# Issuing the first load of a streaming kernel ahead of the program's opening barrier

## The chip, the cores and the metric

The kernel runs on one core of one Trainium2 chip. The metric is the device time of one execution in microseconds (us). A run is one execution of the program. Runs are called fast, or slow when they lie over 1.5% above the fastest run of the same kernel. A ratio below is the mean time of one kernel's fast runs over that of the other's fast runs of the same rounds, so it is not quite the ratio of the medians that are quoted beside it. The profile is one execution; its span is about 2 us shorter than the device time.

## The reference

```python
batch, seq, d_model, r = 16, 512, 768, 16      # x: 16 x 512 x 768 fp32, A: 768 x 16, B: 16 x 768
def reference(x, A, B, scale):                 # scale = 0.5
    lora = np.matmul(np.matmul(x, A), B)
    return (x + scale * lora).astype(np.float32)
```

x is 25.2 MB and so is the output. A and B are 48 KB each.

## The kernel before

x is cut into 8 groups of 3.1 MB (128 partitions of 24,576 bytes). For each group ScalarE casts x to fp16, VectorE transposes it in 32 by 32 blocks of 32-bit words, TensorE multiplies with A (spread into a block-diagonal matrix `a_diag`), ScalarE spreads the result into `y_diag`, TensorE multiplies with B (`b_rep`), and VectorE adds the product to x in place. The tensor goes out from the same buffer. Six buffers hold x. All transfers are issued by SP (SyncE), and so stand in one queue:

```python
    xs = [const.tile([P, G, D], fp32, name=f"x_{i}") for i in range(X_BUFS)]   # X_BUFS = 6
...
    def load(g):
        nc.sync.dma_start(out=xs[g % X_BUFS], in_=view(x2, g)).then_inc(loaded[g], 16)

    def sync_program():
        load(0)
        nc.sync.dma_start(
            out=a32.rearrange("i (b r) -> i b r", b=NB),
            in_=A.rearrange("(b i q) r -> i b (q r)", i=Q, q=2),
        ).then_inc(a_in, 16)
        nc.sync.dma_start(out=b32, in_=B).then_inc(b_in, 16)
        for g in range(1, X_BUFS):
            load(g)
        for g in range(NG - 1):
            nc.sync.wait_ge(added, 4 * (g + 1) + 2)
            nc.sync.dma_start(out=view(out2, g), in_=xs[g % X_BUFS]).then_inc(...)
            if g == len(freed) - 1:
                for n in range(X_BUFS, NG):
                    nc.sync.wait_ge(freed[n - X_BUFS], 16)
                    load(n)
...
    def vector_program():
        ...                                   # A and B to fp16, a_diag, b_rep: waits for a_in and b_in
        turn(0, 0, G // 2)._wait_ge(ready, 1)
        turn(0, G // 2, G // 2)._wait_ge(ready, 2)
        for g in range(NG):
            if g + 1 < NG:
                turn(g + 1, 0, G)._wait_ge(ready, 2 * g + 4)      # the transpose
            for s in range(0, G, 2):
                ...                                               # x += product, four times
...
    with tc.tile_critical(no_gpsimd_drain=True):
        sync_program(); pool_program(); scalar_program(); vector_program(); tensor_program()

    nc.sync.dma_start(out=view(out2, NG - 1), in_=xs[(NG - 1) % X_BUFS])
```

The program begins with a barrier that nobody wrote here: GpSimd sets four constants, every engine reports, and GpSimd releases them. Only then does SP reach `load(0)`.

## Time and profile before

The time before is 124.38 us (median of 4 runs, 124.25 to 124.48).

| What | Before | Where it is read |
|---|---|---|
| SP reaches the barrier / is released | 0.00 / 0.65 us | the records of single instructions in the trace |
| first load issued | 0.94 us, for 0.38 us | timeline |
| first packet of that load | 1.95 us | the DMA packets in the trace |
| first load landed | 11.6 us | the DMA's semaphore in the trace, and ScalarE's wait |
| from one landing to the next | 7.3 us | the same |
| last store issued / stores before it landed | 106.3 / 114.1 us | timeline / semaphore |
| last packet | 121.0 us | the DMA packets |

The profile's page of the kernel before: its span, the busy time of each engine, the granted TensorE clock, the DMA's busy share in tenths and its rate in 40 equal slices, the one queue's share of the 16 engines' span, and the chain of work that ended last.

```profile
span 122.2 us, 888 instructions
PE 50.6 (41%) x323; PEld 30.0 (25%) x323; DVE 84.2 (69%) x48; ACT 55.9 (46%) x42; POOL 4.9 (4%) x9
...
PEclk9999999976999999999999999999999999655555
DMA  5899999999999999999999999999999999999992
GB/s 129 378 459 346 418 451 418 435 435 418 443 426 418 451 426 410 451 451 394 475 418 402 459 426 410 443 435 410 459 418 451 435 410 451 427 402 467 427 410 121
...
q1 hardware_dynamic: 2736, 50.43, 97.2%
...
DVE 44%; PE 21%; DMA 14%; ACT 6%; SPq 1%; issue 1%
```

The queue is busy for 97.2% of the engines' span, and no engine of compute comes near that: VectorE (DVE) has 69%. The last line seems to say otherwise, with VectorE first in the chain that ended last. The timeline of the kernel before, at its start and at its end (start in us, length, engine, line, operation, output<-input; "SPq" is SP's sequencer, that is, the issue of a transfer):

```profile
0.94 0.38 SPq L92 DMA_DIRECT2D x_61<-in_x_dram  x1
1.37 0.43 SPq L96 DMA_DIRECT2D a_71<-in_A_dram  x1
1.85 0.46 SPq L100 DMA_DIRECT2D b_72<-in_B_dram  x1
2.35 0.42 SPq L92 DMA_DIRECT2D x_62<-in_x_dram  x1
...
11.62 5.41 ACT L132 CAST xh_67<-x_61 128x3072 f16<-128x3072 f32 x2 [9.44 <-DMA x_61<-in_x_dram]
```

```profile
104.03 1.75 DVE L186 TENSOR_TENSOR x_62<-x_62,lora_ps_80 128x1536 f32<-128x1536 f32 x1
106.28 0.33 SPq L242 DMA_DIRECT2D out_dram<-x_62  x1
```

SP's own waits in the kernel before (who waited for whom: us in total, times, longest):

```profile
SPq L273 <- DMA out_dram<-x_62: 14.8, 1, 14.8
```

The last store is issued at 106.3 us and SP then waits 14.8 us for it, although one 3.1 MB transfer takes 7.3 us. The other half is queueing: the store before it lands only at 114.1 us, 7.8 us after the last one is issued. So the end hangs on the queue.

### The profile page before, as it was taken

To read this page: it belongs to the slowest core of one execution; us is meant where nothing else is said; L and a number is where in the kernel's file an instruction comes from. 1 tells how busy PE (TensorE), PEld (TensorE's weight loads), DVE (VectorE), ACT (ScalarE), POOL (GpSimd) and SP (SyncE) were. 2 spreads that over 40 slices of the span, in tenths; PEclk is the share of its full clock that TensorE was granted. 3 is DMA by queue.
4 is the path that set the end of the run, shared out by engine and by line. 5 is a ranking of instruction groups with operands and counts; after the bars stand their busy time and mean duration, and the time that the engine had idled before them with its cause. 6 is when DMAs were issued, how large, how long until landed. Compare 5 with 4: busy or idle time off the path is not lost.

```text
span 122.2 us, 888 instructions
## 1 busy us (share of the span) xinstructions
PE 50.6 (41%) x323; PEld 30.0 (25%) x323; DVE 84.2 (69%) x48; ACT 55.9 (46%) x42; POOL 4.9 (4%) x9
## 2 busy tenths in 40 slices
PE   0000406747744674294374458429437545000000
PEld 0000004512531352182153226217214422000000
DVE  0001993099999999999999999999999559600000
ACT  4001956989459629908934099991400310000000
POOL 7800000000000000000000000000000000000000
PEclk9999999976999999999999999999999999655555
DMA  5899999999999999999999999999999999999992
GB/s 129 378 459 346 418 451 418 435 435 418 443 426 418 451 426 410 451 451 394 475 418 402 459 426 410 443 435 410 459 418 451 435 410 451 427 402 467 427 410 121
DMA packets 2736, 50.43 MB, mean 413 GB/s; under 512 B 672, under 2 KB 672, under 8 KB 688
## 3 DMA queue, kind: packets, MB, share of 16 engines
q1 hardware_dynamic: 2736, 50.43, 97.2%
HBM read 25.26 MB, written 25.17 MB: 413 GB/s over the span
## 4 chain that ended last, share of the span: by engine, by line
DVE 44%; PE 21%; DMA 14%; ACT 6%; SPq 1%; issue 1%
DVE xt L155 19%; PE y_ps L213 15%; DMA x_62<-in_x_dram 14%; DVE x_62 L186 8%; DVE x_61 L186 5%; PE lora_ps_80 L227 5%; ACT xh_68 L132 4%; DVE x_66 L186 3%; DVE x_65 L186 3%; DVE x_63 L186 3%; DVE x_64 L186 3%; ACT y_diag L143 1%; PE lora_ps_79 L227 1%; SPq L100 0%; SPq L96 0%
## 5 line engine op out<-in xcount | busy, mean ns | idle before, releaser
L213 PE MATMUL y_ps<-xt,a_diag 128*128 128x256 f16 x192 | 24.2, 282 | 5.9 <-DVE xt L155 5.9
L227 PE MATMUL lora_ps_79<-b_rep,y_diag 128*128 128x512 f16 (+1 forms) x64 | 13.8, 340 | 27.9 <-ACT y_diag L143 14.4
L143 ACT ACTIVATE y_diag<-y_ps 32x256 f16<-32x256 f32 x32 | 12.0, 375 | 25.7 <-PE y_ps L213 25.4
L213 PEld LDWEIGHTS y_ps<-xt,a_diag 128*128 128x128 f16 x192 | 18.9, 99 | 11.1 <-DVE xt L155 6.6
L155 DVE STREAM_TRANSPOSE xt<-xh_68 128x3072 uint32<-128x3072 uint32 x4 | 13.5, 3378 | 6.0 <-ACT xh_68 L132 5.2
L227 PE MATMUL lora_ps_80<-b_rep,y_diag 128*128 128x512 f16 (+1 forms) x64 | 13.8, 340 | 6.7 <-DVE x_61 L186 1.7
L132 ACT CAST xh_67<-x_61 128x3072 f16<-128x3072 f32 (+1 forms) x3 | 10.7, 3603 | 12.6 <-DMA x_61<-in_x_dram 12.6
L155 DVE STREAM_TRANSPOSE xt<-xh_67 128x3072 uint32<-128x3072 uint32 (+1 forms) x5 | 13.6, 2728 | 0.8 <-PE y_ps L213 0.8
L227 PEld LDWEIGHTS lora_ps_79<-b_rep,y_diag 128*128 128x128 f16 x64 | 5.1, 99 | 35.8 <-issue 16.9
L132 ACT CAST xh_68<-x_62 128x6144 f16<-128x6144 f32 x2 | 10.6, 5312 | 2.5 <-DMA x_62<-in_x_dram 2.5
L227 PEld LDWEIGHTS lora_ps_80<-b_rep,y_diag 128*128 128x128 f16 x64 | 5.8, 101 | 13.3 <-DVE x_61 L186 2.5
L186 DVE TENSOR_TENSOR x_62<-x_62,lora_ps_79 128x1536 f32<-128x1536 f32 x4 | 7.0, 1740 | 2.8 <-PE lora_ps_79 L227 2.8
L164 DVE CAST a_74<-a_71 32x384 f16<-32x384 f32 x1 | 0.3, 348 | 11.9 <-DMA a_71<-in_A_dram 11.9
L186 DVE TENSOR_TENSOR x_62<-x_62,lora_ps_80 128x1536 f32<-128x1536 f32 x4 | 7.0, 1744 | 0.0
L186 DVE TENSOR_TENSOR x_61<-x_61,lora_ps_80 128x1536 f32<-128x1536 f32 x4 | 7.0, 1741 | 0.0
L186 DVE TENSOR_TENSOR x_61<-x_61,lora_ps_79 128x1536 f32<-128x1536 f32 x4 | 6.9, 1728 | 0.0
L198 PE MATMUL lora_ps_79<-a_74,rep 32*128 32x384 f16 x1 | 0.5, 497 | 12.3 <-DVE a_74 L164 12.3
L132 ACT CAST xh_67<-x_63 128x6144 f16<-128x6144 f32 x1 | 5.3, 5313 | 0.4 <-DMA x_63<-in_x_dram 0.4
L132 ACT CAST xh_68<-x_64 128x6144 f16<-128x6144 f32 x1 | 5.3, 5312 | 0.0
L132 ACT CAST xh_68<-x_66 128x6144 f16<-128x6144 f32 x1 | 5.3, 5312 | 0.0
L132 ACT CAST xh_67<-x_65 128x6144 f16<-128x6144 f32 x1 | 5.3, 5312 | 0.0
L186 DVE TENSOR_TENSOR x_63<-x_63,lora_ps_80 128x1536 f32<-128x1536 f32 x2 | 3.5, 1742 | 0.0
(23 smaller groups left out, 35.5 us busy)
## 6 DMA issues: line engine op xcount, KB each, us to landing
x_61<-in_x_dram SPq DMA_DIRECT2D x2, 3072.0 KB, 12.6
x_62<-in_x_dram SPq DMA_DIRECT2D x2, 3072.0 KB, 15.8
out_dram<-x_61 SPq DMA_DIRECT2D x2, 3072.0 KB, 19.5
out_dram<-x_62 SPq DMA_DIRECT2D x2, 3072.0 KB, 16.6
x_63<-in_x_dram SPq DMA_DIRECT2D x1, 3072.0 KB, 23.7
x_64<-in_x_dram SPq DMA_DIRECT2D x1, 3072.0 KB, 30.5
x_65<-in_x_dram SPq DMA_DIRECT2D x1, 3072.0 KB, 37.2
x_66<-in_x_dram SPq DMA_DIRECT2D x1, 3072.0 KB, 44.0
```

The costliest lines, as they stand in the source:

```text
L132: i = nc.scalar.copy(out=xh[g % 2][:, rows, :], in_=xs[g % X_BUFS][:, rows, :])
L143: i = nc.scalar.mul(out=y_diag[q, :, q], in_=y_ps[q, :, :], mul=sc)
L155: i = nc.vector.transpose(out=xt[:, rows, :].rearrange("p s w -> p (s w)"), in_=xh[g % 2][:, rows, :].rearrange("p s d -> p (s d)").bitcas ...
L164: nc.vector.tensor_copy(out=a16, in_=a32)._wait_ge(a_in, 16).then_inc(setup_dve, 1)
L186: nc.vector.tensor_tensor(out=rows, in0=rows, in1=lora_ps[n % 2], op=mybir.AluOpType.add)._wait_ge(ups, n + 1).then_inc(added, 1)
L198: nc.tensor.matmul(a_ps, rep, a16, start=True, stop=True)._wait_ge(setup_dve, 1).then_inc(setup_pe, 1)
L213: i = nc.tensor.matmul(y_ps, a_diag[:, k, :], xt_mm[:, :, k // 2, :, k % 2], start=(k == 0), stop=(k == 2 * NB - 1),)
L227: i = nc.tensor.matmul(flat[:, ds(c0, w)], y_diag[:, s + k, :], b_rep[:, ds(c0 - k * D, w)], start=True, stop=True,)
```

## The change

The intent: SP does nothing useful in the opening barrier, and the load of the first group depends on nothing that the barrier orders. So its issue is put in front of SP's part in the barrier. The program's first block is made before the framework places its tiles, so the buffer of that load gets a fixed address of its own.

```diff
-    xs = [const.tile([P, G, D], fp32, name=f"x_{i}") for i in range(X_BUFS)]
+    x_0 = nc.alloc_sbuf_tensor("x_0", [P, G, D], fp32).ap()
+    xs = [x_0] + [const.tile([P, G, D], fp32, name=f"x_{i}") for i in range(1, X_BUFS)]
...
     def sync_program():
+        symbolic, nc._always_lower_symbolic_ap = nc._always_lower_symbolic_ap, False
         load(0)
+        nc._always_lower_symbolic_ap = symbolic
+
+        now, first = nc.cur_bb.bb.instructions, nc.main_func.blocks[0].instructions
+        at = next(
+            k for k, i in enumerate(first)
+            if i.engine == mybir.EngineType.SP and isinstance(i, mybir.InstDrain)
+        )
+        first.insert(at, now.pop())
         nc.sync.dma_start(
             out=a32.rearrange("i (b r) -> i b r", b=NB),
```

## The prediction

> **What bounds the kernel now.** The DMA queue, from end to end. The page gives the DMA digit 9 in 38 of 40 slices, 97.2% of the 16 engines' span, 50.43 MB at 413 GB/s. All loads and stores stand in one queue, and the landings in the trace are a steady beat: the first load of x at 11.6 us, the next ones at 19.2, 26.5, 33.9, 41.2, 48.5, then the first two stores at 55.8 and 63.1, one 3.1 MB transfer per 7.3 us. The packets of that queue run from 1.95 us to 121.02 us with no hole between. The last store is issued at 106.3 us (timeline), when the store before it has not landed (114.1 us), so it stands about 7.8 us behind others. The page's "chain that ended last" (VectorE 44%) therefore misleads: VectorE could finish about 7 us later and the end would not move. The Trainium skill ("DMA: Bandwidth & Descriptors", section on queues, rings and completion order) says that each engine consumes its descriptors in ring order; the landings agree.
>
> **What the change does.** It takes the first load's issue from 0.94 us to the front of the program, before SP's part in the opening barrier. The trace shows SP's first instruction at 0.00 us and the barrier's release reaching SP at 0.65 us, then two small steps and the issue at 0.94 us. The issue takes 0.38 us, and the first packet moves 0.63 us after it ends. (The same page, "Latency and other measured facts", states about 0.6 us for this; the trace agrees.) Nothing is added: the same transfers, sizes and queue. The order of instructions shows only this one moved; the other engines have identical rows. SP now reaches the barrier at about 0.43 us instead of 0.01 us, but GpSimd, which gathers it, is itself ready only at 0.53 us, so I expect the release at 0.61 us to stay, or slip by at most 0.1 us. The loads of A, B and x1 then go out one issue earlier (about 0.43 us); they queue behind x0 anyway.
>
> **On the critical path.** The queue starts about 0.9 us earlier (first packet at about 1.0 us instead of 1.95) and stays full: x0 takes about 8 us to move, and x1 would be issued at about 1.9 us. Every landing should move by the same 0.9 us, and the end too, since all the stores have slack (the last one 7.8 us) and the compute chain starts earlier as well. Gain: 0.94 us at most, about 0.9 us expected, 0.7% of the time.
>
> **Predicted time:** 123.5 us, range 123.1 to 124.1. Faster by over 2%: 0.01; within 2%: 0.98; slower by over 2%: 0.01.
>
> **What would show it.** First packet at about 1.0 us; x0 landed at about 10.7 us, x1 at 18.3; last packet at about 120.1; span about 121.3; the bytes and the mean 7.3 us beat unchanged; the barrier's release still near 0.6 to 0.7 us; VectorE's and ScalarE's busy times unchanged. The wait of the last store, about 14.8 us, stays.
>
> **What would make it wrong.** (a) SP's drain in the barrier waits for the load itself: then the other engines start late, up to about 10 us, and A, B and x1 are issued after x0, a hole in the queue of a microsecond or two: no gain, or a loss. (b) The first packets, which already take 1.85 us against 0.91 later, ramp more slowly so early in the program, and eat half the gain. (c) The load is the first instruction SP runs and begins later than its drain did, so that the clock of the measurement starts with it and the gain shrinks. (d) The gain is only a few times the spread of runs (124.25 to 124.48), so two medians may show 0.5 or 1.2 us.

## The result

The changed kernel takes 123.43 us (median of 4 runs, 123.18 to 123.67) against 124.38 us; the ratio is 0.9924, with a 95% interval of 0.9897 to 0.9951. Repeated on another chip with six runs it took 123.30 us against 124.31 us, ratio 0.9914 (0.9895 to 0.9934). The page of the changed kernel:

```profile
span 121.3 us, 888 instructions
PE 52.1 (43%) x323; PEld 30.6 (25%) x323; DVE 84.2 (69%) x48; ACT 55.9 (46%) x42; POOL 4.9 (4%) x9
...
PEclk9999999965699999999999999999999999975555
DMA  7999999999999999999999999999999999999991
GB/s 227 421 392 419 397 478 413 397 478 421 397 478 405 413 470 413 413 454 430 413 446 438 413 438 446 413 438 438 421 438 438 413 446 438 413 446 438 413 454 73
...
q1 hardware_dynamic: 2736, 50.43, 97.8%
...
DVE 44%; PE 22%; DMA 13%; ACT 6%; SPq 1%; issue 1%
```

The DMA row has moved at its two ends alone: the first 3 us carry 227 GB/s where they carried 129, and the last 3 us carry 73 where they carried 121. The timeline of the changed kernel, at its start and its end, and SP's wait for the last store:

```profile
0.00 0.38 SPq L94 DMA_DIRECT2D x<-in_x_dram  x1
0.99 0.34 SPq L107 DMA_DIRECT2D a_70<-in_A_dram  x1
1.38 0.73 SPq L111 DMA_DIRECT2D b_71<-in_B_dram  x1
2.16 0.41 SPq L94 DMA_DIRECT2D x_61<-in_x_dram  x1
...
10.41 5.41 ACT L143 CAST xh_66<-x 128x3072 f16<-128x3072 f32 x2 [8.18 <-DMA x<-in_x_dram]
```

```profile
103.87 1.75 DVE L197 TENSOR_TENSOR x_61<-x_61,lora_ps_79 128x1536 f32<-128x1536 f32 x1
106.12 0.33 SPq L253 DMA_DIRECT2D out_dram<-x_61  x1
```

```profile
SPq L284 <- DMA out_dram<-x_61: 14.1, 1, 14.1
```

| us from the span's start | Before | After | Earlier by |
|---|---|---|---|
| first load issued | 0.94 | 0.00 | 0.94 |
| first packet | 1.95 | 1.00 | 0.94 |
| x0 landed | 11.59 | 10.39 | 1.20 |
| x1 landed | 19.22 | 18.06 | 1.16 |
| last load of x landed | 77.73 | 76.44 | 1.29 |
| last store but one landed | 114.12 | 113.25 | 0.87 |
| last packet of all | 121.02 | 120.04 | 0.98 |
| last addition on VectorE ended | 105.78 | 105.62 | 0.16 |

The queue moved as a whole by about 0.9 to 1.3 us, and the span became 0.87 us shorter (122.16 and 121.29 us). A landing here is the last of 16 engines (the trace has 16 packets of 4 bytes, for the semaphore, after each transfer), so it carries a few tenths of scatter.

The last row of the table is a small surprise. VectorE's chain began 1.16 us earlier, with ScalarE's cast of the second group, but ended only 0.16 us earlier. The chain of work that ended last shows where it lost its lead. First the kernel before, then the changed one (start, us, what):

```profile
24.59 3.38 DVE xt L155
27.97 3.31 DVE x_61 L186 x2
...
31.33 0.82 PE lora_ps_80 L227 x4
32.15 2.69 PE y_ps L213 x24
```

```profile
23.43 3.38 DVE xt L166
26.81 3.32 DVE x L197 x2
...
30.17 1.46 PE lora_ps_79 L238 x4
31.63 3.05 PE y_ps L224 x24
```

The same matmuls took 1.46 and 3.05 us in place of 0.82 and 2.69, which is 1.0 us. From 30 to 40 us the clock granted to TensorE was 1.00 before and 0.89 after (mean over that stretch): the trace has it at half from 26.04 to 29.45 us before, and from 25.44 to 32.27 us after. (The 9s of the PEclk row before 22 us only mean that no record of the clock stands there.) The Trainium skill's page "TensorE: Matmul & The Clock Gate", part 1, says that the array is throttled by default and that activity releases it, with a phase that varies from run to run; the traces agree in that the half clock lies among the first rounds of matmuls and elsewhere in each (30.27 to 33.69 us in the repeat of the changed kernel below), but no run here shows what sets it. The lead was lost at no cost to the end, as a chain with slack allows. That is the second sign that the chain does not set the end.

### The profile page after: what moved, and what is told of

Read it like the earlier page. It is cut to its first block, busy times and chain, and to the rows that moved or that the text cites. A ratio compares the mean times of both kernels' runs of the same rounds, so it can differ in the third digit from the quotient of the medians.

```text
span 121.3 us, 888 instructions
## 1 busy us (share of the span) xinstructions
PE 52.1 (43%) x323; PEld 30.6 (25%) x323; DVE 84.2 (69%) x48; ACT 55.9 (46%) x42; POOL 4.9 (4%) x9
## 4 chain that ended last, share of the span: by engine, by line
DVE 44%; PE 22%; DMA 13%; ACT 6%; SPq 1%; issue 1%
DVE xt L166 19%; PE y_ps L224 16%; DMA x_61<-in_x_dram 13%; DVE x_61 L197 8%; DVE x L197 5%; PE lora_ps_79 L238 5%; ACT xh_67 L143 4%; DVE x_65 L197 3%; DVE x_63 L197 3%; DVE x_64 L197 3%; DVE x_62 L197 3%; ACT y_diag L154 1%; PE lora_ps_78 L238 1%; SPq L111 1%; SPq L107 0%
## 5 line engine op out<-in xcount | busy, mean ns | idle before, releaser
L224 PE MATMUL y_ps<-xt,a_diag 128*128 128x256 f16 x192 | 24.8, 287 | 5.8 <-DVE xt L166 5.8
L238 PE MATMUL lora_ps_78<-b_rep,y_diag 128*128 128x512 f16 (+1 forms) x64 | 14.1, 346 | 27.9 <-ACT y_diag L154 14.1
L238 PE MATMUL lora_ps_79<-b_rep,y_diag 128*128 128x512 f16 (+1 forms) x64 | 14.4, 351 | 6.1 <-DVE x_61 L197 1.7
L143 ACT CAST xh_66<-x 128x3072 f16<-128x3072 f32 (+1 forms) x3 | 10.7, 3604 | 10.3 <-DMA x<-in_x_dram 10.3
L197 DVE TENSOR_TENSOR x_61<-x_61,lora_ps_78 128x1536 f32<-128x1536 f32 x4 | 7.0, 1741 | 2.8 <-PE lora_ps_78 L238 2.8
L175 DVE CAST a_73<-a_70 32x384 f16<-32x384 f32 x1 | 0.3, 349 | 10.8 <-DMA a_70<-in_A_dram 10.8
L197 DVE TENSOR_TENSOR x_61<-x_61,lora_ps_79 128x1536 f32<-128x1536 f32 x4 | 7.0, 1744 | 0.0
L197 DVE TENSOR_TENSOR x<-x,lora_ps_79 128x1536 f32<-128x1536 f32 x4 | 7.0, 1741 | 0.0
L197 DVE TENSOR_TENSOR x<-x,lora_ps_78 128x1536 f32<-128x1536 f32 x4 | 6.9, 1729 | 0.0
L209 PE MATMUL lora_ps_78<-a_73,rep 32*128 32x384 f16 x1 | 0.5, 496 | 11.2 <-DVE a_73 L175 11.2
L197 DVE TENSOR_TENSOR x_62<-x_62,lora_ps_79 128x1536 f32<-128x1536 f32 x2 | 3.5, 1742 | 0.0
```

The lines of the kernel that those rows point to most:

```text
L143: i = nc.scalar.copy(out=xh[g % 2][:, rows, :], in_=xs[g % X_BUFS][:, rows, :])
L175: nc.vector.tensor_copy(out=a16, in_=a32)._wait_ge(a_in, 16).then_inc(setup_dve, 1)
L197: nc.vector.tensor_tensor(out=rows, in0=rows, in1=lora_ps[n % 2], op=mybir.AluOpType.add)._wait_ge(ups, n + 1).then_inc(added, 1)
L209: nc.tensor.matmul(a_ps, rep, a16, start=True, stop=True)._wait_ge(setup_dve, 1).then_inc(setup_pe, 1)
L224: i = nc.tensor.matmul(y_ps, a_diag[:, k, :], xt_mm[:, :, k // 2, :, k % 2], start=(k == 0), stop=(k == 2 * NB - 1),)
L238: i = nc.tensor.matmul(flat[:, ds(c0, w)], y_diag[:, s + k, :], b_rep[:, ds(c0 - k * D, w)], start=True, stop=True,)
```

## The experiments

The theory (the queue): one DMA queue is full from its first packet to its last, so the end is the first packet plus a constant, and the gain is the 0.94 us by which the first packet came earlier. The rivals: the VectorE chain that ended last sets the end, and gains because x0 is there earlier (the chain); or the buffer's place outside the framework brings part of the gain (the placement).

### The change again, as a yardstick

No edit. The first four runs of the changed kernel lay in two groups (123.18 and 123.23, 123.63 and 123.67 us), so it was repeated.

> The changed kernel once more, as a yardstick on this chip and for the spread. Queue theory (the end is set by one full DMA queue, so the gain is how much earlier its first packet moves, 0.94 us): ratio to before 0.992 to 0.993. If its runs fall into two groups again (123.2 and 123.65 in the first four), the profile of this run tells which part of the queue's time differs.

123.30 us (6 runs, 123.10 to 123.44), ratio 0.9914. The two groups did not come again, so there was nothing to explain.

### The placement alone

```diff
-    xs = [const.tile([P, G, D], fp32, name=f"x_{i}") for i in range(X_BUFS)]
+    x_0 = nc.alloc_sbuf_tensor("x_0", [P, G, D], fp32).ap()
+    xs = [x_0] + [const.tile([P, G, D], fp32, name=f"x_{i}") for i in range(1, X_BUFS)]
```

> The buffer x_0 outside the framework, but the first load issued where it was before. Queue theory: 124.4 us, ratio 0.999 to 1.001, first packet at 1.95 us. Rival (the placement of the buffer itself brings part of the gain): ratio below 0.998.

124.34 us, ratio 1.0001 (0.9980 to 1.0022); the first packet is at 1.95 us. The placement brings nothing, to within the 0.2% of the interval, where the change brings 0.8 to 0.9%: that rival is out.

### The queue's start moved the other way, by five times as much

```diff
     def sync_program():
+        nc.sync.wait_ge(pool_done, 2)
         load(0)
```

> The kernel before, with SP made to wait ahead of its first load until GpSimd has done its setup at 5.76 us, so that the whole queue starts 4.8 to 4.9 us later. Queue theory: time rises by all of it, to 129.2 us (slope 1.0 us per us of start), with the beat between landings unchanged at 7.3 us. If there were slack anywhere between the queue's start and the end, it would rise by less.

129.00 us (4 runs, 128.87 to 129.15), ratio 1.0374 (1.0349 to 1.0399). The first packet came at 6.80 us, 4.85 us later than before, and the time rose by 4.69 us: 0.97 us for each us of start. The page's DMA row of this run shows the empty start and a queue that is full afterwards:

```profile
DMA  0099989999999999999999999999999999999993
```

The expectation was 129.2 us; the 0.2 us that is missing is about the scatter of single runs. This run delays the queue and the chain alike, so it measures the slope and does not tell the two apart. The next two do.

### VectorE made slower, by 3.4 and by 10.1 us

The transpose of the last group is done two times, or four times, the result being the same (`delay` is a semaphore that orders the repeats):

```diff
+                extra = 1 if g + 1 == NG - 1 else 0        # 3 in the second run
+                for k in range(extra):
+                    nc.vector.wait_ge(*((delay, k) if k else (ready, 2 * g + 4)))
+                    nc.vector.transpose(out=xt..., in_=xh[(g + 1) % 2]...).then_inc(delay, 1)
+                if extra:
+                    nc.vector.wait_ge(delay, extra)
                 turn(g + 1, 0, G)._wait_ge(ready, 2 * g + 4)
```

> The changed kernel with VectorE's transpose for the last group done twice: 3.4 us more VectorE work on the chain that the profile says ended last. Queue theory: VectorE's last addition ends at about 109 us, still before the queue gets to the last store (113.3 us), so the time stays at 123.4 us (ratio to before 0.992). Rival (the VectorE chain sets the end): 3.4 us longer, 126.8 us.

123.61 us (4 fast runs, 123.37 to 124.05), ratio 0.9952 (0.9928 to 0.9977). The last addition ended at 110.6 us where it ended at 105.6 in the changed kernel, so 5 us later: 3.4 us for the repeat, the rest in slower rounds of matmuls. The end hardly moved: by 0.3 us against the yardstick, or 0.4% by the two ratios (0.9952 against 0.9914). SP's wait for the last store shrank by the same 5 us, from 14.1 us to this:

```profile
SPq L294 <- DMA out_dram<-x: 9.1, 1, 9.1
```

> The same with that transpose done four times: 10.1 us more VectorE work. Queue theory: the last addition ends at about 115.8 us and the last store is issued at about 116.3 us, 3.1 us after the queue ran empty at 113.2 us and with about 1 us from issue to first packet, so the end moves by about 4 us: 127.4 us. Rival (the VectorE chain sets the end): 10.1 us longer, 133.5 us.

One run was fast, at 127.61 us; three were slow, at 129.54 to 130.04 us. The fast one is 4.3 us over the yardstick (123.30 us), where the queue theory said about 4 and the chain theory 10.1. The profile fell on a slow run, and its chain shows matmuls of the last group at 4.16 us in place of 2.69:

```profile
103.36 1.46 PE lora_ps L248 x4
104.82 4.16 PE y_ps L234 x24
```

The trace has the clock at half from 94.11 to 107.77 us. There is no trace of the fast run to set beside it, so why the others were slower is not settled. With one fast run there is no interval. The two runs together rule out the chain as what bounds the kernel: 5 us of delay were free, and 10.1 us or more cost 4.3. How much slack it has can be estimated from the traces. Where the last store is late (this one, three loads ahead, and A and B later, below), the last packet comes 8.3 us after its issue. In the changed kernel it comes at 120.04 us, so an issue up to 111.7 us should be free; it came at 106.1, which makes some 5.6 us of slack.

### Three loads ahead of the barrier

If one load ahead is good, are three better?

```diff
     # x_0, x_1 and x_2 get fixed addresses
-        load(0)
+        for g in range(3):
+            load(g)
...
-        first.insert(at, now.pop())
+        for g in range(3):
+            first.insert(at, now.pop())
...
-        for g in range(1, X_BUFS):
+        for g in range(3, X_BUFS):
             load(g)
```

> The first three loads of x ahead of the barrier instead of one. Queue theory: the first packet stays at 1.0 us and the queue is full either way, so the time is that of the changed kernel, ratio to before 0.992 (to within 0.002), although SP comes to the barrier about 0.9 us later and all other engines start that much later. Rival (the issue of each load, or the start of the engines, is on the critical path): two more issues of 0.45 us each ahead bring either a further 0.9 us of gain or 0.9 us of loss.

133.11 us (6 runs, 130.78 to 135.17), ratio 1.0576 (1.0521 to 1.0631) from its two fast runs, 130.78 and 132.24 us. No theory expected a loss of some 8 us against the changed kernel (9.8 us by the median, which counts the slow runs). The page's DMA row of this run (a slow one) has holes, one of which is empty for a whole slice in the row of rates, and the timeline shows when VectorE could begin:

```profile
DMA  7999999999999928905999989799999999996885
GB/s 230 446 423 438 438 409 453 357 409 446 431 416 446 394 119 357 475 0 238 475 305 409 453 386 468 275 438 446 423 438 423 438 438 416 438 438 260 357 357 238
```

```profile
25.64 0.35 DVE L177 CAST a<-a 32x384 f16<-32x384 f32 x1 [25.64 <-DMA a<-in_A_dram]
```

A, which stood behind one load of x, now stands behind three. It lands at 25.6 us in place of 10.8, and no group can be finished without it. Two runs tell this apart from the late start of the other engines.

### Four loads ahead, in the old order; and one load ahead, in the new order

The first puts x0, A, B and x1 ahead of the barrier, in that order (with buffers of fixed address for all four). The second keeps only x0 ahead and moves A and B back:

```diff
-        [A and B]
-        for g in range(1, X_BUFS):
-            load(g)
+        load(1)
+        load(2)
+        [A and B]
+        for g in range(3, X_BUFS):
+            load(g)
```

> The run with three loads ahead lost 9 us, which no theory had. Its trace shows A landing at 25.6 us instead of 10.8, behind three loads of x in the queue, and the compute chain starting that much later than its slack of about 7 us allows. So this run puts four loads ahead of the barrier, x0, A, B and x1, in the order that the queue has in the changed kernel. If the order of the queue made the loss: no loss, the changed kernel's time, 123.3 us, ratio to before 0.991 to 0.993, although all other engines start about 1.3 us later. If issuing more ahead of the barrier made it (the late start of the other engines): again several us more.

123.44 us (5 runs, 123.27 to 123.66), ratio 0.9930 (0.9917 to 0.9944): the changed kernel's time, to within the spread. A landed at 11.2 us. GpSimd's and ScalarE's first own work came 1.5 us later than in the changed kernel (ScalarE's table load at 2.44 us in place of 0.95), and it cost nothing.

> The changed kernel (only x0 ahead of the barrier) with A and B issued after x1 and x2 in place of before x1. If the order of the queue made the loss of the run with three loads ahead: A lands at about 25 us again and the time is that run's, 131 to 135 us, with holes in the queue after the six first loads. If the barrier made it: 123.3 us.

One fast run at 130.49 us, three slow at 132.66 to 133.47 us. The fast one lies where the fast runs with three loads ahead lie (130.78 and 132.24), and 7.2 us over the yardstick. So the order in the queue made the loss, and the barrier had no part in it. The sum works out from the trace of this run (a slow one): VectorE starts on A at 25.75 us in place of 10.79, its first addition at 41.6 in place of 26.7, and the last store is issued at 121.4 us in place of 106.1. Its turn in the changed kernel's queue came at 113.2 us, so it is 8.2 us overdue, and with about 1 us from issue to first packet the end should be about 9.2 us later. The last packet of this run is at 129.75 us, 9.7 us later than the changed kernel's. The fast run lost 2.3 us less; it has no trace. The timeline:

```profile
25.75 0.35 DVE L177 CAST a<-a 32x384 f16<-32x384 f32 x1 [25.75 <-DMA a<-in_A_dram]
...
121.42 0.33 SPq L255 DMA_DIRECT2D out_dram<-x  x1
```

### A and B one place later

> The changed kernel with A and B issued after x1 only, one transfer later than it has them and one earlier than the run that lost 9 us. If the slack of the compute chain (last store issued at 106.1 us, its turn in the queue at 113.2 us) decides: A lands at about 18.3 us, VectorE's first addition starts about 5.4 us later than in the changed kernel (32 us in place of 26.8), its last one ends at about 111 us, still ahead of the queue: no loss, 123.3 us, ratio to before 0.992. If every place later costs, about half of that run's 9 us.

The edit is the same with `load(1)` alone ahead of A and B. One run was fast, at 123.35 us, which is the changed kernel's time; three were slow, at 125.52 to 126.02 us. The profile fell on a slow one. Its chain shows the first two rounds of matmuls, then a round of full speed:

```profile
25.98 5.32 PE y_ps L225 x24
...
39.41 3.80 PE y_ps L225 x24
...
50.80 2.69 PE y_ps L225 x24
```

A landed at 18.4 us as expected, but the first addition began at 34.6 us and not at 32, because the first of these rounds took 5.32 us in place of 2.69. In this trace the last store was issued at 114.7 us, 3 us past the 111.7 us estimated above, and the last packet came 3 us later than in the changed kernel. But the store before it had landed late as well, at 115.2 us in place of 113.3: the queue carried only 0.60 MB from 60 to 62 us and 0.61 from 76 to 78, where 0.86 is its rate. So the late issue is not the whole of it. What the runs show is that one place later can be free; why three of four lost some 2 us is left open, as the only trace is of a slow run.

### Trying for more: A and B on another queue, and A in longer runs

After the change the queue has one visible loss left: where A and B pass. Counted from the packets of the changed kernel, it moves 1.53 MB from 8 to 12 us, where 4 us at its steady rate carry 1.72 MB.

```diff
     # ScalarE issues A and B, ahead of its part in the barrier; SP issues x alone
     # (a32 and b32 get fixed addresses, here and in the last attempt)
-        nc.sync.dma_start(out=a32..., in_=A...).then_inc(a_in, 16)
-        nc.sync.dma_start(out=b32, in_=B).then_inc(b_in, 16)
...
     def scalar_program():
+        nc.scalar.dma_start(out=a32..., in_=A...).then_inc(a_in, 16)
+        nc.scalar.dma_start(out=b32, in_=B).then_inc(b_in, 16)
+        ...                                     # both moved ahead of ScalarE's drain
```

> The changed kernel with the loads of A and B issued by ScalarE, ahead of the barrier too. Queue theory: the same bytes and packets pass the same 16 engines, so at first sight no change; if the small packets fall into the start, where the first packets of x0 take 1.7 us instead of 0.91 us[...], part of their 0.4 us is hidden: between 0 and 0.4 us less than the changed kernel. A rival expects a loss[...].

133.39 us (6 runs, 131.26 to 133.94), ratio 1.0621 (1.0564 to 1.0678) from three fast runs. A was issued at 0.13 us and landed at 25.6 us. The DMA issues of this run (engine, count, KB each, median us from issue to landing):

```profile
a<-in_A_dram ACTq DMA_DIRECT2D x1, 48.0 KB, 25.5
b<-in_B_dram ACTq DMA_DIRECT2D x1, 48.0 KB, 26.1
```

The Trainium skill's page "DMA: Bandwidth & Descriptors", in its section on queues, rings and completion order, says that each engine takes turns between the queues that have work, packet by packet. The trace agrees on the turns. But the page counts some 9 to 17 descriptors to a packet, and the turns here were smaller: A is 384 packets of 128 bytes in the profile, 24 for each of the 16 engines. They move from 3.4 to 23.8 us, 0.85 us apart on one engine on average, and one packet of x takes 0.91 us (the small packets of x's own semaphores are turns too). So each 128 bytes waited for 24,576. In one queue, behind x0, the same packets passed in about 1 us.

```diff
     # VectorE's transpose takes its columns with a stride, so that a partition of A is one run
-            in_=A.rearrange("(b i q) r -> i b (q r)", i=Q, q=2),
+            in_=A.rearrange("(i b q) r -> i b (q r)", i=Q, q=2),
...
-            out=xt[:, rows, :].rearrange("p s w -> p (s w)"),
-            in_=xh[g % 2][:, rows, :].rearrange("p s d -> p (s d)").bitcast(u32),
+            out=xt[:, rows, :].rearrange("p s (b i) -> p s b i", b=NB),
+            in_=xh[g % 2][:, rows, :].bitcast(u32).rearrange("p s (i b) -> p s b i", b=NB),
```

> The changed kernel with A loaded as one run of 1536 bytes per partition (32 packets) in place of 384 packets of 128 bytes; the transpose reads its columns with a stride to match. In the trace of the changed kernel the queue moves 0.757 MB between 8 and 10 us where 0.863 MB is its steady amount, and falls short once more by about 0.09 MB just after, so the small packets cost about 0.4 us. Queue theory: 0.3 to 0.4 us less than the changed kernel, 123.0 us, ratio to before 0.989 to 0.990, even if the strided transpose is slower on VectorE, as long as it is below about 4.3 us each. If the strided transpose takes far longer, VectorE sets the pace and the time rises.

146.33 us (7 runs), ratio 1.1667 (1.1638 to 1.1696) from four fast runs: a miss. With the stride the transposes took 44.9 us in all in place of 27 (5.6 us for a whole group in place of 3.4), the groups of this run say, a slow one. VectorE also sat idle for 18.1 us before them, waiting for matmuls, in place of 2.6; the mean granted clock was 0.82 in place of 0.91. So the chain through VectorE and TensorE set the pace:

```profile
L166 DVE STREAM_TRANSPOSE xt<-xh 128x3072 uint32<-128x3072 uint32 (+1 forms) x9 | 44.9, 4992 | 18.1 <-PE y_ps L224 18.1
```

And the queue lost about as much as before where A and B passed: it moved 1.55 MB from 8 to 12 us. So the small packets of A were not what cost. The last attempt puts the stride into ScalarE's cast, and A (in runs of 1536 bytes) and B on ScalarE's queue:

```diff
-        i = nc.scalar.copy(out=xh[g % 2][:, rows, :], in_=xs[g % X_BUFS][:, rows, :])
+        i = nc.scalar.copy(
+            out=xh[g % 2][:, rows, :].rearrange("p s (b i q) -> p s b i q", b=NB, q=2),
+            in_=xs[g % X_BUFS][:, rows, :].rearrange("p s (i b q) -> p s b i q", b=NB, q=2),
+        )
```

> A and B issued by ScalarE ahead of the barrier, as in the run that lost 8 us, but A as one run of 1536 bytes per partition: 2 packets for each engine in place of 24. In the lost run A landed at 25.6 us, which fits two queues taking turns packet by packet (24 turns of 0.91 us are 22 us). If so, A and B land by about 5 us here, and the loss is gone. The stride that matches this order of A sits in ScalarE's cast this time, not in VectorE's transpose (which went from 3.4 to 5.0 us with it). With A and B out of the way of the queue of x, whose trace falls short by 0.19 MB between 8 and 12 us where they pass, up to 0.4 us less than the changed kernel: 122.9 to 123.3 us, ratio to before 0.988 to 0.992, if the strided cast stays under about 10 us; if not, ScalarE sets the pace.

123.41 us (5 runs, 123.31 to 123.53), ratio 0.9922 (0.9908 to 0.9935): the changed kernel's time. The loss of 8 us is gone, as turns of a few packets would have it:

```profile
a<-in_A_dram ACTq DMA_DIRECT2D x1, 48.0 KB, 6.7
b<-in_B_dram ACTq DMA_DIRECT2D x1, 48.0 KB, 8.6
```

(A landed at 6.8 us and B at 9.2; I had left out that the queue's first turn comes only at 3.5 us and that the semaphore write takes a turn as well.) ScalarE's cast of a group took 7.8 us in place of 5.3, under the limit of about 10. (The 5.0 us for the transpose in the expectation is a mean over whole and half groups; a whole group took 5.6.) The hoped gain did not come. The packets of x next to those of A and B took 1.0 to 1.3 us in place of 0.91 here too, only at 6 to 8 us in place of 9 to 10. From 4 to 14 us the engines fell short of their steady rate by 0.22 MB here and by 0.19 MB in the changed kernel. So passing A and B costs some 0.4 to 0.5 us of the queue wherever they stand; why packets of x beside them slow down is left open. No version here beats the changed kernel.

## Why the prediction was right

The number: 123.5 us was predicted, with 123.1 to 124.1 as the range, and 123.43 us was measured. Point by point:

- "What bounds the kernel now: the DMA queue, from end to end." Right. 3.4 us more VectorE work left the time within 0.4% of the changed kernel, and 4.85 us more of queue start cost 4.69 us. (One reading in it was off: the DMA row has a 9 in 37 slices, not in 38.)
- "The chain that ended last misleads; VectorE could finish about 7 us later." Right in kind, and about 1 us too much. The 7.8 us leave out the time from issue to first packet; by the 8.3 us from a late issue to the last packet the slack was about 6.4 us before and 5.6 us after the change. 5 us later was free; 10.1 us or more cost 4.3.
- "First packet at about 1.0 us": 1.00. "x0 landed at about 10.7, x1 at 18.3": 10.39 and 18.06. "Last packet at about 120.1; span about 121.3": 120.04 and 121.29.
- "SP reaches the barrier at 0.43 us; the release stays or slips by at most 0.1 us": SP's drain began at 0.43 us and took 0.13 us in place of 0.01; the release at SP slipped from 0.65 to 0.70 us. The drain did not wait for the load, which landed 10 us later, so fear (a) was unfounded. Nor did the start of the span move: zero is by definition the program's first instruction, which is SP's in both traces, but GpSimd's first memset comes 0.23 us after it in both, so (c) fell as well. (b): the first 16 packets took 1.56 us on average, against 1.65 before, so they were no slower.
- "The 0.63 us from the issue's end to the first packet" held: 0.38 to 1.00 us, 0.62 us.
- "The compute chain starts earlier as well" is true of its start (1.16 us), but it ended only 0.16 us earlier, because two rounds of matmuls met a lower clock. "The wait of the last store, about 14.8 us, stays" was off by that: 14.1 us.

What the prediction did not see is the other side of its own argument. In a first-in-first-out queue the start of the queue is worth its full time, and so is the order in it: the expectation for the run with three loads ahead repeated "the queue is full either way" and was wrong by some 8 us, because A and B had moved back.

## What to carry to other kernels

Where one DMA queue is full from end to end, expect time saved before its first packet to be saved whole, as the 0.94 us were here; find such a queue by comparing the issue of the last store, and the 1 us or so to its first packet, with the landing of the one before, not by the chain that ended last. What can be issued without waiting for anything belongs ahead of the opening barrier, but small inputs that everything depends on must keep their place near the front, and a second queue beside a stream of large packets was no way to hurry them when they consisted of many small packets.

## What the Trainium skill lacked or had wrong

- "DMA: Bandwidth & Descriptors", section "Issuing engines are not separate DMA queues", says that issuing from several engines only saves issue time. It lacks that it can cost: the 384 packets of A on a queue of their own landed at 25.6 us, behind x0 on the shared queue at 10.8 us, and the kernel lost 6% (ratio 1.0621). With 2 packets for each engine in place of 24 it landed at 6.8 us and the loss was gone.
- The same page has nothing on what a small transfer costs its neighbours in a full queue: packets of x next to A and B took 1.1 to 1.3 us in place of 0.91, with 128-byte and with 1536-byte runs alike.
- The same page, "Latency and other measured facts", states about 0.6 us to the first byte, but not from when it counts: the runs have 0.63 and 0.62 us from the end of the issue, and 1.00 us from its start.
- "VectorE: DVE Perf Modes", section "The DRAIN you can't avoid", says that the drains which the runtime puts before and after a kernel, on all engines, take a constant 12 ns or so. It lacks the drain of the program's own barrier behind a DMA: SP's took 7 ns with nothing ahead of it, but 131 ns behind a load. It did not wait for the load, which landed 10 us later. No page that I read has the cost of the program's own opening barrier: SP was released 0.65 us after its start.
- "SBUF — State Buffer", section on the DMA port swizzle, says that accesses which step past a 16-byte line pay a penalty, without its size for these engines. The runs agree and have one: with a step of 48 bytes on its input VectorE's 32-bit transpose of a group rose from 3.4 to 5.6 us, and with a step of 96 bytes between pairs of words on its input ScalarE's cast of a group rose from 5.3 to 7.8 us.
